# State-space output products four in a row, a contiguous tap table, whole-block input turns and kept low parts in a two-layer encoder trunk

## The chip, the core and the metric

The kernel runs on one core of a Trainium2 chip. Its engines work side by side and meet through semaphores: TensorE (PE) multiplies matrices into PSUM, VectorE (DVE), ScalarE (ACT) and GpSimd (POOL) do elementwise work, and SyncE (SP) issues the DMAs, in order, on one queue. The metric is the device time of one execution in microseconds (us); lower is better.

## What is computed

A trunk of two layers over a sequence of 1024 tokens with 1024 channels, all in float32. Layer 0 mixes tokens by an RWKV-7 recurrence (16 heads of 64), layer 1 by a diagonal complex state-space layer (S5; 64 groups of 16 channels, each with 64 complex states); each is followed by a dense MLP with squared ReLU, and after each of the four sub-layers the input is added with a factor and normalised. Cut to what matters here:

```python
def rwkv7_time_mix(x, ...):
    ...
    return (o.astype(x.dtype) * g) @ wo

def s5_mix(x, ...):
    ...
    def chunk_step(h, u_c):
        bu_re = jnp.einsum('tbgc,gpc->tbgp', u_c, bbar_re)
        bu_im = jnp.einsum('tbgc,gpc->tbgp', u_c, bbar_im)
            ...
        y = (jnp.einsum('tbgp,gcp->tbgc', s_re, cr_w)
             - jnp.einsum('tbgp,gcp->tbgc', s_im, ci_w))
        return (s_re[-1], s_im[-1]), y
    ...
    y = jax.nn.gelu(y + xf * d_skip)
    z = y @ w_glu
    return z[..., :d] * jax.nn.sigmoid(z[..., d:])

def sq_relu_mlp(x, w1, w2):
    return jnp.square(jax.nn.relu(x @ w1)) @ w2

for i in range(2):
    mix = rwkv7_time_mix(h, ...) if i == 0 else s5_mix(h, ...)
    h = layer_norm(DN_ALPHA * h + mix, ...)
    h = layer_norm(DN_ALPHA * h + sq_relu_mlp(h, ...), ...)
```

## The kernel before

**Layout and halves.** Activations lie with channels on the 128 partitions: 8 channel blocks of 128 (`KT`), and time along the free axis. The sequence is worked in two halves of 512 tokens (`HT`), H = 0 (tiles `hA`, operands `oAh`, `oAl`) and H = 1 (`hB`, `oBh`, `oBl`), so that one half's slow stages stand beside the other half's dense products.

**Dense products.** A float32 operand is split in a high part, rounded by a cast on ACT (L148), and a low part, the difference, on DVE (L149); each product is three PE instructions, high x high, high x low, low x high (`mm3`, issued at L188). `wload` (L162) brings 512 weight columns at a time: a load of 256 KB on SP into `wraw` (two buffers), the split into `whi` and `wlo` (three buffers each), and then 12 PE instructions use them. If a key is given, the first use stores the low part in DRAM (`low`, L180), and a later use loads it (L174) in place of the subtraction. The first half's projections in layer 0 do this for the second half's; the output projection `wo` (L950) has no key.

**Order.** The program is written stage by stage; a planner then orders each engine's instructions by a simulated timeline and by rank, a lower number first. The two MLPs of a half are written with a high number (from 200000), and the state-space layer with 99300 to 99500, so that the dense products of the other half's MLP fill what the state-space layer leaves free. The order on each engine is fixed when the kernel is built. PSUM has four pools with one 2 KB tile each per buffer: `pd` (three, dense products), `pl` (one), `pa` (two), `pc` (two).

**Tables.** `s5_tables` (L1026) makes, once, for each channel block `f` (8 groups in 4 pairs `g2`, two members `par`): `tB` (input to state), `tC` (state to output) and `tT`, the taps inside a stretch of 8 tokens. The taps of one block come from PE into `p` (L1151), ACT copies them into a zero-padded tile `kpad` (L1155), which holds (t, c, g), the pair index innermost, and two DMAs (L1159), one for each `par`, write the 8 shifted copies to `tT`.

**The state-space layer** `s5(H, h)` (L1173) has three stages.

- Input (L1180 to L1207). For a pair of channel blocks (`f2`, members `j`) the tokens are turned onto partitions: for each of 8 token positions `s` a block of 128 channels x 64 stretches is turned, by a transpose for `j` = 0 (L156) and a product with the identity for `j` = 1 (L154), both through `turn`, with every eighth token as the stationary operand. ACT copies to `u1`. Then, group by group, a transpose (L1195) brings (position, channel) onto partitions, ACT copies to `ug`, and products with `tB` (L1206) make the state inputs `hb`.
- Scan (L1209 to L1231): `advance` on DVE and POOL.
- Output (L1235 to L1268). For a pair of blocks the tables `tt` and `tcm` of both blocks are loaded into the four buffers of tag `tab`. For each `par`, one PSUM tile takes 8 tap products (L1250, 128 rows, moving operand `tv`, every fourth float of `tt`) and 16 state products (L1255, 64 rows given by `par`, 64 columns given by `j`); ACT copies it to `y1` (L1257). Transposes (L1263, into `pyt` of pool `pa`) turn it back, DVE adds the skip term (L1265), ACT applies the GELU (into `yg`, one buffer), and a DMA stores it for `glu`.

`glu` (L1007) then reads it back, and the next normalisation and MLP follow.

## Time and profile before

| | |
|---|---|
| median of 3 runs | 2742.12 us |
| lowest, highest | 2735.79, 2742.68 us |
| the profiled execution | 2746.6 us |
| its span, first to last instruction | 2744.8 us |
| mean granted clock of TensorE | 0.961 |

The profile is of one execution; instruction durations in the text are from it. A row of a timeline gives the start, the length from first start to last end, the engine, line, operation, operands (output <- inputs), the part of the array used (rows*columns), the shape, and the count. PE's instructions overlap, so the cost of a block of them is read from its start to the start of the next block. `PEld` is a weight load that runs beside products; `SPq` is a DMA issued by SP. A line such as "A <- B: 5.2, 2, 2.9" means that A waited for B 5.2 us in all, in 2 waits, 2.9 us the longest.

### The profile page before, as it was taken

To read this page: it belongs to the slowest core of one execution; us is meant where nothing else is said; L and a number is where in the kernel's file an instruction comes from. 1 tells how busy PE (TensorE), PEld (TensorE's weight loads), DVE (VectorE), ACT (ScalarE), POOL (GpSimd) and SP (SyncE) were. 2 spreads that over 40 slices of the span, in tenths; PEclk is the share of its full clock that TensorE was granted. 3 is DMA by queue.
4 is the path that set the end of the run, shared out by engine and by line. 5 is a ranking of instruction groups with operands and counts; after the bars stand their busy time and mean duration, and the time that the engine had idled before them with its cause. 6 is when DMAs were issued, how large, how long until landed. Compare 5 with 4: busy or idle time off the path is not lost.

```text
span 2744.8 us, 43807 instructions
## 1 busy us (share of the span) xinstructions
PE 2598.4 (95%) x16582; PEld 2089.9 (76%) x16582; DVE 1813.3 (66%) x3191; ACT 1154.8 (42%) x2038; POOL 630.6 (23%) x515
## 2 busy tenths in 40 slices
PE   7999979989899999989999999999999999999997
PEld 5778757678677777767876788778778887788886
DVE  7477677577786867997567553674855546755556
ACT  7455574544543333353532332434223324433334
POOL 3121542432442122342122000120220101210101
PEclk9989979999899999999999999999999999999998
DMA  4765455564223334545333533233343322333333
GB/s 146 235 214 175 151 164 156 178 203 142 81 86 88 93 92 148 141 129 163 100 112 127 174 95 100 81 96 112 103 164 110 96 96 81 119 96 96 96 96 100
DMA packets 215058, 345.90 MB, mean 126 GB/s; under 512 B 21184, under 2 KB 75584, under 8 KB 214848
## 3 DMA queue, kind: packets, MB, share of 16 engines
q1 hardware_dynamic: 214848, 343.10, 40.5%
q8 instruction: 131, 2.15, 0.3%
q14 instruction: 79, 0.65, 0.1%
HBM read 279.06 MB, written 63.96 MB: 125 GB/s over the span
## 4 chain that ended last, share of the span: by engine, by line
PE 44%; DVE 4%; issue 3%; DMA 1%; POOL 1%; ACT 1%; ACTq 0%; SPq 0%; DVEq 0%; POOLq 0%
PE d L188 39%; PE py L1250 1%; PE py L1255 1%; DVE wlo L149 1%; DMA wraw<-in_mw_dram 1%; PE pu L154 1%; PE pbu L1206 1%; POOL rl L975 1%; DVE hA L991 0%; DMA s_y<-yg 0%; DVE t L1218 0%; DVE hB L991 0%; ACT whi L148 0%; DVE sq L876 0%; PE pu L1195 0%
## 5 line engine op out<-in xcount | busy, mean ns | idle before, releaser
L148 ACT CAST whi<-wraw 128x512 fp32r<-128x512 f32 x668 | 413.5, 620 | 929.1 <-PE d L188 623.2
L149 DVE TENSOR_TENSOR wlo<-wraw,whi 128x512 fp32r<-128x512 f32 x668 | 500.6, 750 | 426.8 <-ACT whi L148 404.3
L188 PE MATMUL d<-qbuf,whi 128*128 128x512 f32 (+1 forms) x2112 | 657.0, 394 | 23.8 <-DVE hA L991 12.8
L188 PEld LDWEIGHTS d<-qbuf,whi 128*128 128x128 f32 x2112 | 391.8, 191 | 120.0 <-DVE hA L991 17.8
L188 PE MATMUL d<-qbuf,wlo 128*128 128x512 f32 (+1 forms) x1056 | 411.9, 392 | 10.7 <-DVE wlo L149 10.4
L975 POOL TENSOR_TENSOR rl<-rl 128x512 f32<-128x512 f32 x128 | 157.2, 1228 | 1094.5 <-ACT rl L974 1094.5
L188 PE MATMUL d<-oAh,whi 128*128 128x512 f32 (+1 forms) x960 | 390.9, 411 | 15.5 <-ACT ev L418 6.3
L188 PE MATMUL d<-oAl,whi 128*128 128x512 f32 (+1 forms) x960 | 387.5, 405 | 3.0 <-DVE oAl L149 2.8
L188 PE MATMUL d<-oAh,wlo 128*128 128x512 f32 (+1 forms) x960 | 386.5, 405 | 2.4 <-DVE wlo L149 2.3
L188 PE MATMUL d<-oBh,whi 128*128 128x512 f32 x704 | 279.2, 397 | 0.0
L188 PE MATMUL d<-oBh,wlo 128*128 128x512 f32 x704 | 278.7, 396 | 0.2 <-DVE wlo L149 0.2
L188 PE MATMUL d<-oBl,whi 128*128 128x512 f32 x704 | 277.1, 394 | 0.0
L188 PEld LDWEIGHTS d<-qbuf,wlo 128*128 128x128 f32 x1056 | 201.7, 191 | 56.5 <-DVE wlo L149 14.5
L188 PEld LDWEIGHTS d<-oAh,whi 128*128 128x128 f32 (+1 forms) x960 | 185.9, 194 | 62.2 <-ACT ev L418 8.4
L188 PEld LDWEIGHTS d<-oAh,wlo 128*128 128x128 f32 (+1 forms) x960 | 185.8, 194 | 44.4 <-DVE wlo L149 3.2
L188 PEld LDWEIGHTS d<-oAl,whi 128*128 128x128 f32 (+1 forms) x960 | 185.6, 194 | 43.1 <-DVE oAl L149 5.2
L991 DVE TENSOR_TENSOR hB<-hB,d 128x512 f32<-128x512 f32 (+1 forms) x256 | 165.0, 650 | 71.2 <-PE d L188 68.0
L991 DVE TENSOR_TENSOR hA<-hA,d 128x512 f32<-128x512 f32 x240 | 162.1, 682 | 64.4 <-PE d L188 62.1
L188 PEld LDWEIGHTS d<-oBh,wlo 128*128 128x128 f32 x704 | 132.9, 189 | 32.4 <-issue 2.0
L188 PEld LDWEIGHTS d<-oBl,whi 128*128 128x128 f32 x704 | 133.1, 189 | 29.9 <-issue 0.7
L188 PEld LDWEIGHTS d<-oBh,whi 128*128 128x128 f32 x704 | 133.1, 189 | 29.0 <-issue 1.2
L149 DVE TENSOR_TENSOR qbuf<-rl,qbuf 128x512 fp32r<-128x512 f32 x128 | 95.0, 742 | 73.5 <-ACT qbuf L148 73.5
(374 smaller groups left out, 3804.8 us busy)
## 6 DMA issues: line engine op xcount, KB each, us to landing
wraw<-in_mw_dram SPq DMA_DIRECT2D x520, 256.0 KB, 2.7
wraw<-in_glu_dram SPq DMA_DIRECT2D x64, 256.0 KB, 2.7
low<-wlo SPq DMA_DIRECT2D x52, 256.0 KB, 2.6
wlo<-low SPq DMA_DIRECT2D x52, 256.0 KB, 3.6
wraw<-in_wk_dram SPq DMA_DIRECT2D x32, 256.0 KB, 3.5
wraw<-in_wr_dram SPq DMA_DIRECT2D x32, 256.0 KB, 3.9
wraw<-in_wv_dram SPq DMA_DIRECT2D x32, 256.0 KB, 4.3
yl<-s_y SPq DMA_DIRECT2D x32, 256.0 KB, 3.1
```

The source lines that it names most:

```text
L148: S.copy(hi, src)
L149: (e or V).tensor_sub(lo, src, hi.bitcast(F32))
L154: PE.matmul(out, x, idt, start=True, stop=True)
L188: bulk.append((PE.matmul(p, w, x, **kw).ins, x.shape[-1]))
L975: G.tensor_mul(r, r, r)
L991: V.tensor_add(z, z, p)
L1206: PE.matmul(p[qs, g2, ri], tb[:, g2, ri, qs], u[:, 2 * g2 + par], start=True, stop=True)
L1250: PE.matmul(p[64 * j : 64 * j + 64, g2], ug[f][:, 2 * g2 + par], tv[:, par, g2], start=g2 == 0, stop=False, skip_group_check=True)
L1255: PE.matmul(p[64 * j : 64 * j + 64, g2], hb[qs, 4 * f + g2, ri, 0:NSC], tcm[qs, g2, ri], start=False, stop=ri == 1, skip_group_check=True)
```

## The change

Four things are changed.

1. Output products: for each pair of blocks the two `par` now have a PSUM tile each (one of pool `pc`, one of `pa`), all 16 tap products come first, and the 32 state products follow in an order in which `par` changes fastest, then `j`; `inorder` fixes that order for the planner. The turn back, `pyt`, goes to pool `pl`.
2. Tap table: `kpad` becomes two tiles of four blocks each, with the pair index outside, and `tT` is laid out so that the 128 taps of a group lie side by side. The stores come after every fourth block, 16 DMAs then.
3. Input: one block of 128 channels is turned four times as a whole, every fourth token as the stationary operand (128 of them), all by transposes; the second turn becomes two products per group, with the even and the odd columns of the identity (`sel`), each to one half of the PSUM partitions.
4. `wo` gives its weights a key, so the first half stores the low parts and the second half loads them.

```diff
--- before.py
+++ after.py
@@ -31,6 +31,7 @@
 LNG = (1, 3, 5)
 LNT = (2, 5)
 TB = 2
+TBF = 4
 LN8R = 400000
 MIXR = 100
 W0B = 5
@@ -126,6 +127,8 @@
     cmask = kp.tile([128, 8, L], F32, name="cmask")
     V.memset(cmask, 1.0)
     V.memset(cmask[:, :, 0:1], 0.0)
+    sel = cp.tile([128, 2, 64], F32, name="sel")
+    V.tensor_copy(sel, ident.rearrange("p (n e) -> p e n", e=2))
     mhalf = cp.tile([128, 64], F32, name="mhalf")
     V.memset(mhalf, -0.5)
 
@@ -180,6 +183,12 @@
                     SP.dma_start(low[key, k0], lo.bitcast(F32).rearrange("p k n -> p (k n)"))
             out += [(hi[:, k], lo[:, k]) for k in range(step)]
         return out
+
+    def inorder(prods):
+
+        for x, y in zip(prods, prods[1:]):
+            tc.add_manual_dep(y.ins, x.ins.name, mybir.DependencyInfo(
+                mybir.DependencyClass.NoSync, mybir.DependencyReason.DATA), reason="order")
 
     bulk, hops = [], []
     ST = getattr(nc, STE)
@@ -953,7 +962,7 @@
         hs = []
         for n in range(KT):
             p = psd()
-            dense(p, wload(A["wo"][n], KT, 128), ys)
+            dense(p, wload(A["wo"][n], KT, 128, f"wo{n}"), ys)
             h = htile(H)
             SP.dma_start(h, A["xT"][n * 128 : (n + 1) * 128, t0 : t0 + HT])
             V.scalar_tensor_tensor(h, h, ALPHA, p, op0=ALU.mult, op1=ALU.add)
@@ -1019,7 +1028,7 @@
 
     SL = 8
     NSC = HT // SL
-    tT = dr.tile([KT, 128, 2, 512], F32, name="tT")
+    tT = dr.tile([128, 2, KT, 4, 128], F32, name="tT")
     tB = dr.tile([KT, 128, 4, 2, 128], F32, name="tB")
     tC = dr.tile([KT, 128, 4, 2, 128], F32, name="tC")
 
@@ -1102,10 +1111,12 @@
         V.tensor_sub(ci, ci, tq)
         V.tensor_mul(ci, ci, den)
 
-        kpad = pp.tile([128, 16, 16, 4], F32, name="kpad")
-        G.memset(kpad, 0.0)
+        kpads = [pp.tile([128, TBF, 4, 16, 16], F32, name=f"kpad{j}") for j in range(KT // TBF)]
+        for kpad in kpads:
+            G.memset(kpad[:, :, :, 0:8], 0.0)
         for f in range(KT):
             gs = slice(4 * f, 4 * f + 4)
+            kpad = kpads[f // TBF]
             bc = pp.tile([128, 2, 2, 4, 16], F32, tag="bc", name="bc", bufs=1)
             SP.dma_start(bc, A["s5bc"][f])
             bb = pp.tile([128, 2, 4, 16], F32, tag="bb", name="bb", bufs=1)
@@ -1152,11 +1163,13 @@
                                   ca[ps_, g2, ri, 0:8].rearrange("p t c -> p (t c)"), start=ri == 0, stop=ri == 1)
             for par in range(2):
                 ps_ = slice(64 * par, 64 * par + 16)
-                S.copy(kpad[ps_, 8:].rearrange("p t c g -> p g (t c)"), p[ps_])
-            tv = tT[f].rearrange("(s c) two n -> two c s n", c=16)
-            for par in range(2):
-                src = kpad[64 * par : 64 * par + 16, 1:9].rearrange("p t c g -> p (t c g)")
-                SP.dma_start(tv[par], bass.AP(src.tensor, src.offset, [src.ap[0], (64, SL), src.ap[1]]))
+                S.copy(kpad[ps_, f % TBF, :, 8:].rearrange("p g t c -> p g (t c)"), p[ps_])
+            if f % TBF == TBF - 1:
+                for par in range(2):
+                    for s in range(SL):
+                        SP.dma_start(
+                            tT[16 * s : 16 * s + 16, par, f - TBF + 1 : f + 1].rearrange("c f g n -> c (f g) n"),
+                            kpad[64 * par : 64 * par + 16, :, :, 1 + s : 9 + s].rearrange("c f g t e -> c (f g) (t e)"))
 
             bs = pp.tile([128, 4, 2, 128], F32, tag="bs", name="bs", bufs=1)
             for hf in range(2):
@@ -1178,21 +1191,21 @@
             V.tensor_copy(hb[:, :, :, 0], carry[0])
         ug = []
         for f2 in range(4):
-            u1 = s5p.tile([128, 8, SL, 16], F32, tag="u1", name="u1", bufs=2)
-            for s2 in range(2):
+
+            u1 = s5p.tile([128, 2, 8, 4, 16], F32, tag="u1", name="u1", bufs=2)
+            for j in range(2):
                 p = pa.tile([128, 4, 128], F32, tag="a", name="pu1")
-                for j in range(2):
-                    src = h[2 * f2 + j].rearrange("p (c s) -> p c s", s=SL)
-                    for s in range(4):
-                        turn(p[64 * j : 64 * j + 64, s], src[:, :, SL - 1 - 4 * s2 - s], ident, j)
-                S.copy(u1[:, :, 4 * s2 : 4 * s2 + 4].rearrange("p g s c -> p s g c"),
-                       p.rearrange("p s (g c) -> p s g c", g=8))
+                src = h[2 * f2 + j].rearrange("p (m s) -> p s m", s=4)
+                for s in range(4):
+                    PE.transpose(p[:, s], src[:, 3 - s], ident)
+                S.copy(u1[:, j].rearrange("p g s c -> p s g c"), p.rearrange("p s (g c) -> p s g c", g=8))
             for j in range(2):
                 f = 2 * f2 + j
-                ps_ = slice(64 * j, 64 * j + 64)
                 p = pc.tile([128, HT], F32, tag="c", name="pu2").rearrange("p (g n) -> p g n", g=8)
                 for g in range(8):
-                    PE.transpose(p[:, g], u1[ps_, g].rearrange("p s c -> p (s c)"), ident[ps_, ps_])
+                    for e in range(2):
+                        PE.matmul(p[64 * (1 - e) : 64 * (1 - e) + 64, g], u1[:, j, g].rearrange("p s c -> p (s c)"),
+                                  sel[:, e], start=True, stop=True)
                 u = s5p.tile([128, 8, NSC], F32, tag="ug", name="ug", bufs=8)
                 S.copy(u, p)
                 ug.append(u)
@@ -1237,28 +1250,34 @@
             tabs = []
             for f in (2 * f2, 2 * f2 + 1):
                 tt = s5p.tile([128, 2, 512], F32, tag="tab", name="tt", bufs=4)
-                SP.dma_start(tt, tT[f])
+                SP.dma_start(tt.rearrange("p two (g n) -> p two g n", g=4), tT[:, :, f])
                 tcm = s5p.tile([128, 4, 2, 128], F32, tag="tab", name="tcm", bufs=4)
                 SP.dma_start(tcm, tC[f])
-                tabs.append((f, tt.rearrange("p two (n g) -> p two g n", g=4), tcm))
+                tabs.append((f, tt.rearrange("p two (g n) -> p two g n", g=4), tcm))
+
+
+            pp = [r.tile([128, HT], F32, tag=t, name="py").rearrange("p (g n) -> p g n", g=4)
+                  for r, t in ((pc, "c"), (pa, "a"))]
+            for g2 in range(4):
+                for par in range(2):
+                    for j, (f, tv, tcm) in enumerate(tabs):
+                        PE.matmul(pp[par][64 * j : 64 * j + 64, g2], ug[f][:, 2 * g2 + par], tv[:, par, g2],
+                                  start=g2 == 0, stop=False, skip_group_check=True)
+            prods = []
+            for g2 in range(4):
+                for ri in range(2):
+                    for j, (f, tv, tcm) in enumerate(tabs):
+                        for par in range(2):
+                            qs = slice(64 * par, 64 * par + 64)
+                            prods.append(PE.matmul(pp[par][64 * j : 64 * j + 64, g2], hb[qs, 4 * f + g2, ri, 0:NSC],
+                                                   tcm[qs, g2, ri], start=False, stop=ri == 1, skip_group_check=True))
+            inorder(prods)
             for par in range(2):
-                qs = slice(64 * par, 64 * par + 64)
-                p = pc.tile([128, HT], F32, tag="c", name="py").rearrange("p (g n) -> p g n", g=4)
-
-                for g2 in range(4):
-                    for j, (f, tv, tcm) in enumerate(tabs):
-                        PE.matmul(p[64 * j : 64 * j + 64, g2], ug[f][:, 2 * g2 + par], tv[:, par, g2],
-                                  start=g2 == 0, stop=False, skip_group_check=True)
-                for g2 in range(4):
-                    for ri in range(2):
-                        for j, (f, tv, tcm) in enumerate(tabs):
-                            PE.matmul(p[64 * j : 64 * j + 64, g2], hb[qs, 4 * f + g2, ri, 0:NSC], tcm[qs, g2, ri],
-                                      start=False, stop=ri == 1, skip_group_check=True)
-                S.copy(y1[:, :, :, par].rearrange("p t g c -> p g t c"), p.rearrange("p g (t c) -> p g t c", t=SL))
+                S.copy(y1[:, :, :, par].rearrange("p t g c -> p g t c"), pp[par].rearrange("p g (t c) -> p g t c", t=SL))
             for j in range(2):
                 f = 2 * f2 + j
                 js = slice(64 * j, 64 * j + 64)
-                p = pa.tile([128, SL, NSC], F32, tag="a", name="pyt")
+                p = pl.tile([128, HT], F32, tag="l", name="pyt").rearrange("p (t n) -> p t n", t=SL)
                 for t in range(SL):
                     PE.transpose(p[:, t], y1[js, t].rearrange("p g r c -> p (g r c)"), ident[js, js])
                 y = s5p.tile([128, HT], F32, tag="yg", name="yg", bufs=1)
```

## The prediction

> **What bounds the kernel now.** I read the page first (one core, so no comparison of cores), then a table of stages (busy time of each engine in stretches that I cut at the state-space layer), then TensorE's order of work inside those stretches, then the waits.
>
> ```profile
> span 2744.8 us, 43807 instructions
> PE 2598.4 (95%) x16582; PEld 2089.9 (76%) x16582; DVE 1813.3 (66%) x3191; ACT 1154.8 (42%) x2038; POOL 630.6 (23%) x515
> ```
>
> TensorE is busy for 95% of the span, 146.4 us idle; VectorE follows at 66%. A share is an average, so the stages decide. Columns of the table: stretch in us from the span's start, its length, busy us (and instructions) of PE, its weight loads, DVE, ACT, POOL, then granted clock, DMA share, GB/s.
>
> ```profile
> 1115.00:1270.00 155.00, 138.31 (x763) 104.63 (x762) 145.69 (x235) 67.00 (x102) 62.41 (x44) 0.93 0.54 142
> 1327.00:1403.00 76.00, 76.00 (x630) 61.59 (x629) 36.02 (x54) 33.24 (x57) 4.91 (x5) 1.00 0.35 108
> 1403.00:1481.00 78.00, 70.35 (x297) 53.35 (x295) 66.96 (x113) 20.06 (x34) 26.22 (x14) 0.96 0.30 95
> 1481.00:1545.00 64.00, 64.00 (x544) 48.93 (x544) 29.90 (x41) 23.02 (x38) 7.68 (x5) 0.99 0.65 223
> 1545.00:1660.00 115.00, 114.88 (x504) 94.09 (x503) 61.55 (x95) 37.39 (x64) 11.10 (x11) 1.00 0.34 99
> ```
>
> For the first half of the sequence: 1115 to 1270 builds the tables and finishes the second half's output projection, and there DVE is the full engine (145.69 of 155). 1327 to 1403 turns the input into groups, 1403 to 1481 is the scan (DVE 66.96 of 78), 1481 to 1545 makes the output `py`. In the input and output stretches PE is not idle, and in the 115 us after them only for 0.12: dense products of the MLP (L188) fill every hole, and the work behind is more of the same. So PE work removed from the input and output stretches shortens the run one for one; PE work removed from the scan becomes idle time. The second half repeats the three stretches some 530 us later.
>
> **The output products.** PE's order of work for one pair of channel blocks (start, length, line):
>
> ```profile
> 1489.03 0.65 PE L1250 MATMUL py<-tt,ug 128*64 128x128 f32 x2
> 1489.60 1.01 PE L1263 MATMUL pyt<-ident,y 64*128 64x64 f32 x16
> 1490.55 2.01 PE L1250 MATMUL py<-tt,ug 128*64 128x128 f32 x14
> 1492.49 1.96 PE L1255 MATMUL py<-tcm,hb 64*64 64x128 f32 x32
> 1494.38 2.01 PE L1250 MATMUL py<-tt,ug 128*64 128x128 f32 x16
> 1496.33 1.96 PE L1255 MATMUL py<-tcm,hb 64*64 64x128 f32 x32
> 1498.22 0.51 PE L188 MATMUL d<-oBh,whi 128*128 128x512 f32 x1
> ```
>
> The loops call 16 tap products (L1250) and 32 state products (L1255) for such a pair; the trace has 32 and 64, so one fp32 product is two PE instructions. From one start to the next block's start, the pair costs 0.57 us (1489.03 to 1489.60) and 7.67 us (1490.55 to 1498.22): 8.24 us. There are 4 pairs in each half, 8 in all.
>
> *State products.* 32 instructions take 1.89 us, 0.059 us each. They use 64 rows and 64 columns of the array, a quarter; the two blocks `j` alternate between column halves, the row half (`par`) stays for a whole block of 32. The change alternates rows too, with one PSUM tile per row half. Does PE then run four at once? Once in each half two blocks of L1255 follow each other directly, and a table of L1255 alone around the seam (stretch, length, PE busy and instructions, clock, DMA share, GB/s) shows it:
>
> ```profile
> 1482.10:1482.52 0.42, 0.42 (x12) 1.00 0.75 283
> 1482.80:1483.22 0.42, 0.42 (x20) 1.00 0.17 44
> ```
>
> Inside a block 12 instructions touch 0.42 us; where the end of one row half meets the start of the other, 20. Four are in flight under each 269 ns long instruction in the outer rows (a start each 0.055 us), so 4 of the counted 12 began earlier; at the seam twice the starts fall into the same time. So I price L1255 at half: 64 x 0.0295 = 1.9 us instead of 3.8.
>
> *Tap products.* L1250 uses all 128 rows and 64 columns, its two blocks also alternate columns, yet 16 instructions take 1.95 us, 0.122 each, twice as long as L1255's with the same 128 moving columns. What differs is that the moving table is read at every fourth float. The duration agrees, and the contiguous neighbour with the same 128 rows is L1206 (64 moving columns, two column halves):
>
> ```profile
> L1255 PE MATMUL py<-tcm,hb x512: 269/269/473, 1481.2 to 2057.2; 64*64 64x128 f32 x171
> L1250 PE MATMUL py<-tt,ug x256: 388/406/422, 1401.4 to 2055.1; 128*64 128x128 f32 x128
> 1343.73 2.09 PE L1206 MATMUL pbu<-ug,tb 128*64 128x64 f32 x64
> 1345.74 0.50 PE L188 MATMUL d<-oBl,whi 128*128 128x512 f32 x1
> ```
>
> L1206: 2.01 us / 64 = 0.031 for 64 columns, so 0.063 for 128. With the table contiguous I take 0.059 for L1250: 32 x 0.059 = 1.9 us. The bounds are 0.122 (no gain) and 0.055.
>
> The pair then costs 3.8 us instead of 8.24: 4.45 x 8 = 35.6 us of PE. But some of L1250 is run early, inside the scans, as fill (the same table, of L1250 alone):
>
> ```profile
> 1403.00:1481.00 78.00, 3.84 (x28) 0.96 0.30 95
> 1932.00:2010.00 78.00, 4.08 (x30) 0.96 0.30 97
> ```
>
> Half of 7.92 us saved there turns into idle time: 4.0. **Output products: -31.6 us.**
>
> **The input turn.** One of 8 chunks of a half now takes 4 transposes (L156) and 4 products (L154, 8 instructions):
>
> ```profile
> 1347.93 0.60 PE L156 MATMUL pu<-ident,hA 128*64 128x128 f32 x4
> 1348.46 1.23 PE L154 MATMUL pu<-ident,hA 128*64 128x128 f32 x8
> 1349.62 0.50 PE L188 MATMUL d<-qbuf,whi 128*128 128x512 f32 x1
> ...
> 1322.76 0.64 PE L888 MATMUL pr<-ident,rb 128*128 128x128 f32 x4
> 1323.15 0.48 PE L188 MATMUL d<-qbuf,whi 128*128 128x512 f32 x1
> ```
>
> That is 1.69 us x 8 = 13.5 us a half. The change makes 32 full transposes of strided blocks. No row shows one: four full contiguous ones (L888) take 0.39 us, 0.098 each; four strided ones that load half as many columns (L156) 0.53 us, 0.13 each. If the strided load sets that 0.13, twice the columns make it 0.26. I take 0.13, the strided row: 4.2 us a half, -9.3 (bounds -10.4 and -5.2). Both halves: **-18.6 us.**
>
> The second turn gets dearer: 16 transposes for a pair of blocks become 32 products, 64 instructions, of just L1206's form (2.01 us).
>
> ```profile
> 1337.99 1.01 PE L1195 MATMUL pu<-ident,u 64*128 64x64 f32 x16
> ```
>
> Sixteen of this form take 0.95 us from start to start (L1263 above, 1489.60 to 1490.55, is the same form). 2.01 - 0.95 = 1.06 us for each of 8 pairs: **+8.5 us.** It lies in the full stretch and is paid. ACT's copies are as many as before.
>
> **The way out and the tables.** `pyt` moves to a pool with one buffer, so its second set of transposes waits for VectorE's 1.2 us on the first.
>
> ```profile
> L1265 DVE SCALAR_TENSOR_TENSOR yg<-hA,pv,pyt x8: 1164/1188/1266, 1490.3 to 1539.9; 128x512 f32<-128x512 f32 x8
> ```
>
> PE can put dense products between, as it does everywhere in this stretch; if it can't, 8 x 1.19 = 9.5. I take +1.5, near zero, for the two sets that now run apart. The table stores, 16 now, become 32 of half the size in two bursts of 16, each at 0.36 us on SP's queue, in front of weight loads (in the second row the last number is us from issue to landing):
>
> ```profile
> L1159 SPq DMA_DIRECT2D tT<-kpad x16: 320/362/1264, 1128.6 to 1268.9; - x16
> tt<-tT SPq DMA_DIRECT2D x16, 512.0 KB, 4.2
> ```
>
> A burst holds SP 5.8 us, about two weight loads' worth of dense work; +1 (0 to 11.6). ACT's copies behind them write contiguous rows now, off the path. The table loads (4.2 us) stay of the same size, but the output stretch that carries them is shorter, so they crowd: 223 GB/s over 64 us are 14.3 MB, now in about 48 us, 298 GB/s. Holding the 283 of the first seam row would cost 2.5 us a half; I take +2 for both (0 to 5; all of it at 223, a rival).
>
> **The output projection.** The first half stores 16 low parts (16 more DMAs on SP), the second loads them in place of 16 subtractions on VectorE. Columns: count | busy, mean ns | idle; and for waits total us, times, longest.
>
> ```profile
> L149 DVE TENSOR_TENSOR wlo<-wraw,whi 128x512 fp32r<-128x512 f32 x13 | 11.0, 847 | 0.0
> ...
> PE d L188 <- DVE wlo L149: 5.2, 2, 2.9
> ...
> SPq L174 <- PE d L188: 62.8, 29, 9.9
> SPq L180 <- DVE wlo L149: 47.4, 23, 6.8
> ...
> PE d L188 <- DMA wlo<-low: 0.5, 1, 0.5
> ```
>
> The first row is 1115 to 1165, where this projection meets the tables on the full DVE, the second PE's wait there in 1115 to 1270. I take the 5.2 us that PE visibly waits: **-5** (bounds: 0, and the 11.0 of DVE work). The last three are whole-span rows of the 52 weights that do this already: SP stands still at a load until PE frees a buffer, at a store until DVE is done, and weight loads queue behind; but PE lost only 0.5 us to it. Stores in the first half: +1 (0 to 5).
>
> **Sum:** -31.6 - 18.6 + 8.5 + 1.5 + 1 + 2 - 5 + 1 = -41.2 us. The profiled execution took 2746.6 us (span 2744.8 and 1.8 around it), 4.5 above the median of the runs shown; I subtract from the median: 2742.1 - 41.2 = **2701 us**.
>
> **The rivals.**
> 1. *Products stay in strict order.* If a tile's second instruction holds up the next tile's first, four in a row run as two: +1.9 x 8 = 15, 2716. The seam (20 against 12) speaks against it, so 0.08. [...]
> 2. *The stride is not what slows the tap products.* Then L1250 stays at 0.122: +2 x 8 = 16, 2717. L1206's 0.031 speaks against.
> 3. *Tables and weights don't come fast enough.* If the output stretch can't beat the 223 GB/s measured there, 14.3 MB take their 64 us again and all 16 us a half come back: 2733. For it: the buffers hold one pair's tables, so each pair waits for its loads (4.2 us). Against: the DMA share is 0.65 there, so 298 GB/s would be 0.87, and a short stretch showed 283.
> 4. *The order is planned anew and the gain is given back* in the attention core, where PE has idle time already: 2736, no change. Nothing in the profile points there, but every part of the order may move.
> 5. *Slower: SP's queue.* 32 new waits like the last rows': 16 stores at 47.4/23 = 2.1 us and 16 loads at 62.8/29 = 2.2, all passed on to PE, make 68 us: 2701 + 68 + 5 = 2774. It decides from about 46 us, two thirds of that. Against: the 0.5 us.
>
> **How the numbers follow.** Forecast (2686 to 2712) 0.65; rivals 0.08, 0.07, 0.08, 0.05, 0.07. The range leaves out rivals 3 to 5 (0.20) and takes in the bounds of the turns, the table bursts and the small terms: 2682 to 2724. About 0.3% (8 us) is what a measurement of this kernel can tell from no change: so 2733 lies on the edge and counts half to either side: faster 0.65 + 0.15 + 0.04 = 0.84, same 0.09, slower 0.07.
>
> **What would show it.** The pair of output blocks takes about 3.8 us of PE; L1255 starts four instructions each 0.11 us; L1250's median falls from 406 ns towards L1255's 269; the output stretches shrink by some 15 us each with PE still full; the input stretch by about 5; PE's busy time falls by some 40 us and its idle time hardly. PE idle inside the output stretch would speak for rival 3, waits on `low` for rival 5. I'd be wrong first of all if PE's idle time, 146.4 us, grew by as much as its work shrank.

## The result, and the profile after

| | before | after |
|---|---|---|
| median of the runs, us | 2740.39 (6 runs) | 2759.88 (6 runs) |
| ratio to before, 95% interval | | 1.0071 (1.005 to 1.0091) |
| profiled execution, us (span) | 2746.6 (2744.8) | 2759.87 (2758.2) |

The changed kernel is slower by 0.5 to 0.9%. The forecast was 2701 us (2682 to 2724): the side and the range were both wrong. In the experiments below, one execution of e16 (2884 us at granted clock 0.826) and one of the kernel before beside it (4923 us) were in a slow state and are left out of the ratio. (In this part line numbers are the changed kernel's: dense products L188 are now L197, state products L1255 are L1272, tap products L1250 are L1264, the table store L1159 is L1170, the weight load is L172 and the load of a low part L177. The experiments shift some by a few lines; the tiles' names stay.)

The page of the changed kernel:

```profile
span 2758.2 us, 44350 instructions
...
PE 2568.4 (93%) x16838; PEld 2078.2 (75%) x16838; DVE 1808.8 (66%) x3176; ACT 1146.0 (42%) x2038; POOL 624.6 (23%) x516
```

TensorE's busy time fell from 2598.4 to 2568.4 us, so the work did shrink; its idle time (span less busy) grew from 146.4 to 189.8. The 30.0 us won went into idle time and 13.4 more with them. This is the case that the prediction named as the first that would make it wrong.

Where PE's work shrank, TensorE's order of work in the changed kernel shows (start, length, line; idle time before it in brackets):

```profile
1354.84 1.12 PE L1200 MATMUL pu<-ident,hA 128*128 128x128 f32 x8
1357.17 1.15 PE L1207 MATMUL pu<-sel,u 128*64 128x64 f32 x32 [1.21 <-ACT u L1201]
1358.25 0.72 PE L197 MATMUL d<-qbuf,whi 128*128 128x512 f32 x2
...
1498.14 1.98 PE L1272 MATMUL py<-tcm,hb 64*64 64x128 f32 x64
1500.05 0.74 PE L197 MATMUL d<-qbuf,whi 128*128 128x512 f32 x2
...
1507.54 1.96 PE L1264 MATMUL py<-tt,ug 128*64 128x128 f32 x28
1509.43 0.43 PE L1272 MATMUL py<-tcm,hb 64*64 64x128 f32 x2
1509.79 0.71 PE L1282 MATMUL pyt<-ident,y 64*128 64x64 f32 x8
1510.43 1.97 PE L1272 MATMUL py<-tcm,hb 64*64 64x128 f32 x62
```

A pair's 64 state products take 1.91 us from start to the next start, 28 tap products 1.89 (0.0675 each, 2.16 for the 32). The pair's products cost 4.07 us where they cost 8.24: 4.17 x 8 = 33.4 us less. Eight whole-block transposes take 1.12 us (their length, since PE is idle behind them), 0.14 each: 64 of them 9.0 us in place of 27.0. The second turn takes 1.08 us for 32, 2.16 for a pair in place of 0.95: 9.7 us more; `pyt` 0.64 for 8, 1.28 in place of 0.95: 2.6 more. Sum -39.1 us, close to what was predicted for these parts.

Where the time went, two rows of the table of stages show, cut into 1100 to 1330 us (tables and output projection) and 1330 to 2100 (state-space layers of both halves). The columns are those of the prediction's table: stretch, length, then busy us and instructions of PE, weight loads, DVE, ACT, POOL, then clock, DMA share, GB/s. Before:

```profile
1100.00:1330.00 230.00, 210.97 (x1095) 163.18 (x1094) 205.72 (x346) 97.26 (x153) 80.73 (x58) 0.96 0.49 136
1330.00:2100.00 770.00, 753.18 (x4390) 598.61 (x4389) 458.42 (x699) 271.40 (x463) 126.43 (x89) 0.99 0.37 117
```

After:

```profile
1100.00:1330.00 230.00, 183.66 (x959) 139.30 (x958) 171.22 (x296) 72.50 (x125) 67.16 (x51) 0.91 0.52 146
1330.00:2100.00 770.00, 734.34 (x4710) 594.44 (x4709) 480.18 (x716) 282.28 (x482) 129.23 (x96) 0.98 0.36 117
```

PE's idle time (length less busy) grew from 19.0 to 46.3 us in the first stretch and from 16.8 to 35.7 in the second. In the first, the timeline of SP in the changed kernel shows the two bursts of table stores:

```profile
1162.98 0.41 SPq L172 DMA_DIRECT2D wraw<-in_mw_dram  x1
1163.44 19.41 SPq L1170 DMA_DIRECT2D tT<-kpad  x16
1182.95 1.33 SPq L1181 DMA_DIRECT2D tB<-bs  x1
...
1258.46 19.30 SPq L1170 DMA_DIRECT2D tT<-kpad  x16
1277.86 1.21 SPq L1181 DMA_DIRECT2D tB<-bs  x1
```

A burst of 16 stores holds SP 19.4 us, 1.2 each, not the 5.8 of the forecast. No weight load leaves SP in that time, and the waits of TensorE in 1100 to 1330 us (total us, times, longest) show who pays: a split that waits for its weights, and a low part behind the burst.

```profile
PE d L197 <- ACT whi L151: 22.8, 3, 20.7
PE d L197 <- DMA wlo<-low: 11.3, 1, 11.3
```

In the last 10 us of the second burst nothing runs at all but the stores (table of stages of the changed kernel):

```profile
1268.00:1277.80 9.80, 0.00 (x0) 0.00 (x0) 0.00 (x0) 0.00 (x0) 0.00 (x0) 0.50 0.75 101
```

The DMA engines are 75% busy there and move only 101 GB/s; in the output stretch they are 66% busy and move 230 (row 1498 to 1560, shown below). The engines are occupied, but with stores that go slowly.

In the second stretch the waits of TensorE (1330 to 2100 us) after the change are

```profile
PE py L1264 <- DMA tt<-tT: 10.6, 4, 3.2
PE d L197 <- DVE hB L1000: 9.3, 5, 4.0
PE d L197 <- DVE hA L1000: 8.9, 5, 4.0
PE pu L1207 <- ACT u L1201: 3.1, 2, 1.9
```

and before

```profile
PE d L188 <- DVE wlo L149: 5.3, 3, 2.2
PE d L188 <- DVE hA L991: 4.4, 6, 1.2
PE d L188 <- DVE hB L991: 4.0, 7, 1.1
```

The tap products now wait for their table, and dense products wait twice as long for VectorE's additions. Three stretches of the first half, to set beside the rows of before (input, scan, output):

```profile
1352.00:1420.00 68.00, 66.79 (x726) 55.09 (x726) 32.32 (x49) 32.46 (x55) 4.19 (x4) 1.00 0.37 117
1420.00:1498.00 78.00, 70.28 (x326) 55.79 (x322) 69.31 (x114) 20.05 (x34) 21.46 (x13) 0.93 0.29 92
1498.00:1560.00 62.00, 55.01 (x541) 43.50 (x541) 33.26 (x44) 23.60 (x40) 9.32 (x6) 0.94 0.66 230
```

The output stretch, full before (64.00 of 64.00), now has 7.0 us of idle time.

### The profile page after: what moved, and what is told of

Same layout as the page of the kernel before. It is cut to its first block, busy times and chain, and to the rows that moved or that the text cites. A ratio compares the mean times of both kernels' runs of the same rounds, so it can differ in the third digit from the quotient of the medians.

```text
span 2758.2 us, 44350 instructions
## 1 busy us (share of the span) xinstructions
PE 2568.4 (93%) x16838; PEld 2078.2 (75%) x16838; DVE 1808.8 (66%) x3176; ACT 1146.0 (42%) x2038; POOL 624.6 (23%) x516
## 4 chain that ended last, share of the span: by engine, by line
PE 56%; DVE 14%; DMA 6%; issue 5%; ACT 3%; POOL 2%; SPq 2%; ACTq 0%; DVEq 0%; POOLq 0%
PE d L197 50%; DVE wlo L152 2%; SPq L1170 1%; DMA wraw<-in_mw_dram 1%; PE pA L605 1%; DMA yl<-s_y 1%; DMA ldr<-s_r 1%; DMA s_y<-yg 1%; DVE hA L1000 1%; PE pu L1207 1%; ACT whi L151 1%; PE pbu L1219 1%; DVE xh L650 1%; DVE qbuf L152 1%; DVE x L648 1%
## 5 line engine op out<-in xcount | busy, mean ns | idle before, releaser
L151 ACT CAST whi<-wraw 128x512 fp32r<-128x512 f32 x652 | 404.1, 620 | 942.0 <-PE d L197 692.0
L152 DVE TENSOR_TENSOR wlo<-wraw,whi 128x512 fp32r<-128x512 f32 x652 | 492.6, 757 | 420.2 <-ACT whi L151 403.9
L197 PE MATMUL d<-qbuf,whi 128*128 128x512 f32 (+1 forms) x2112 | 659.1, 395 | 32.2 <-DVE hA L1000 16.0
L197 PEld LDWEIGHTS d<-qbuf,whi 128*128 128x128 f32 x2112 | 394.3, 192 | 127.0 <-DVE hA L1000 24.2
L197 PE MATMUL d<-oAh,whi 128*128 128x512 f32 (+1 forms) x960 | 393.3, 413 | 38.6 <-ACT whi L151 21.1
L197 PE MATMUL d<-qbuf,wlo 128*128 128x512 f32 (+1 forms) x1056 | 412.5, 393 | 5.8 <-DVE wlo L152 5.6
L984 POOL TENSOR_TENSOR rl<-rl 128x512 f32<-128x512 f32 x128 | 147.9, 1156 | 1147.9 <-ACT rl L983 1143.6
L197 PE MATMUL d<-oAl,whi 128*128 128x512 f32 (+1 forms) x960 | 388.3, 406 | 2.2 <-DVE oAl L152 2.0
L197 PE MATMUL d<-oAh,wlo 128*128 128x512 f32 (+1 forms) x960 | 387.1, 406 | 1.2 <-DVE wlo L152 1.2
L197 PE MATMUL d<-oBh,wlo 128*128 128x512 f32 x704 | 278.9, 397 | 11.3 <-DMA wlo<-low 11.3
L197 PE MATMUL d<-oBh,whi 128*128 128x512 f32 x704 | 279.8, 397 | 0.0
L197 PE MATMUL d<-oBl,whi 128*128 128x512 f32 x704 | 277.9, 395 | 0.0
L197 PEld LDWEIGHTS d<-oAh,whi 128*128 128x128 f32 (+1 forms) x960 | 186.6, 195 | 84.5 <-ACT whi L151 22.0
L197 PEld LDWEIGHTS d<-qbuf,wlo 128*128 128x128 f32 x1056 | 202.6, 192 | 50.8 <-DVE wlo L152 8.9
L197 PEld LDWEIGHTS d<-oAl,whi 128*128 128x128 f32 (+1 forms) x960 | 186.9, 195 | 42.7 <-DVE oAl L152 4.3
L197 PEld LDWEIGHTS d<-oAh,wlo 128*128 128x128 f32 (+1 forms) x960 | 186.2, 194 | 42.9 <-DVE wlo L152 1.9
L197 PEld LDWEIGHTS d<-oBh,wlo 128*128 128x128 f32 x704 | 133.3, 189 | 44.3 <-DMA wlo<-low 11.9
L197 PEld LDWEIGHTS d<-oBl,whi 128*128 128x128 f32 x704 | 133.4, 189 | 30.2 <-issue 1.3
L197 PEld LDWEIGHTS d<-oBh,whi 128*128 128x128 f32 x704 | 133.5, 190 | 28.1 <-issue 0.6
```

The source lines that it names most:

```text
L151: S.copy(hi, src)
L152: (e or V).tensor_sub(lo, src, hi.bitcast(F32))
L197: bulk.append((PE.matmul(p, w, x, **kw).ins, x.shape[-1]))
L984: G.tensor_mul(r, r, r)
```

## The experiments

Two theories at first. **The stores**: the two bursts of table stores hold up the weights, and cost some 28 us. **The products**: something in the new order of products or in the kept low parts (the prediction's rival 5) costs it. PE's idle time in the table is worked out as above from two rows of the table of stages of each run.

| kernel | median, us | ratio to before (95%) | PE idle 1100-1330 | 1330-2100 |
|---|---|---|---|---|
| e1 all but the table part | 2732.95 | 0.9976 (0.9961 to 0.999) | 22.2 | 25.1 |
| e4 table part alone | 2760.23 | 1.0084 (1.0057 to 1.0112) | 39.3 | 22.3 |
| e5 four products in a row alone | 2739.89 | 1.0 (0.9988 to 1.0013) | 19.5 | 30.4 |
| e6 whole-block turns alone | 2736.95 | 0.9986 (0.9971 to 1.0) | 21.7 | 18.7 |
| e7 kept low parts alone | 2736.96 | 1.0 (0.9982 to 1.0018) | 22.9 | 15.9 |
| e2 bursts of half the size | 2735.15 | 0.9997 (0.9985 to 1.001) | 27.0 | 37.7 |
| e11 stores issued by POOL | 2753.16 | 1.0041 (1.0025 to 1.0057) | 37.0 | 39.2 |
| e16 halves on two queues | 2746.85 | 1.0019 (1.0002 to 1.0036) | 39.6 | 37.2 |
| e17 halves alternate | 2743.89 | 1.0001 (0.9984 to 1.0018) | 33.7 | 37.8 |
| e3 taps contiguous by 16, stores as before | **2723.87** | **0.9938 (0.9916 to 0.996)** | 21.9 | 34.5 |
| e12 e3, `tt` ahead of `tcm` | 2724.68 | 0.9936 (0.9923 to 0.9948) | 21.9 | 35.0 |
| e15 e12, `pyt` in two buffers | 2732.42 | 0.998 (0.9967 to 0.9993) | 20.1 | 40.0 |
| e13 e3, `yg` from shared buffers | 2853.6 | 1.0409 (1.0395 to 1.0424) | 24.8 | 146.1 |
| e14 e12 and e13 together | 2837.95 | 1.0342 (1.0326 to 1.0359) | 24.8 | 125.8 |

**Which part costs.** e1 is the changed kernel with the table of before: tile, stores and load.

```diff
-            if f % TBF == TBF - 1:
-                for par in range(2):
-                    for s in range(SL):
-                        SP.dma_start(tT[16 * s : 16 * s + 16, par, f - TBF + 1 : f + 1]..., kpad[...])
+            tv = tT[f].rearrange("(s c) two n -> two c s n", c=16)
+            for par in range(2):
+                src = kpad[64 * par : 64 * par + 16, 1:9].rearrange("p t c g -> p (t c g)")
+                SP.dma_start(tv[par], bass.AP(src.tensor, src.offset, [src.ap[0], (64, SL), src.ap[1]]))
```

> The change without its table part: the strided table of before, stored after every block in two DMAs; the other three parts stay. Theory A (the two bursts of 16 table stores hold back the weight loads): the 28 us lost between 1160 and 1300 come back and the tap products cost their 16 us again, 2760 - 28 + 16 = 2748 us. Theory B (the waits of the output projection's kept low parts on SP's queue do it): the loss stays and the taps cost more, about 2776 us.

e4 is the opposite, the kernel before with the table part alone (the same diff the other way round); e7 has the kept low parts alone:

```diff
-            dense(p, wload(A["wo"][n], KT, 128), ys)
+            dense(p, wload(A["wo"][n], KT, 128, f"wo{n}"), ys)
```

> Before with the table part alone (contiguous taps, two bursts). Theory A: 2740 + 28 - 16 (tap products at half) = 2752 us, PE idle between 1160 and 1300 as in the changed kernel. Theory B: no loss there, 2724 us.

> Before with the kept low parts of the output projection alone. Theory A: 2735 to 2741 us, as the prediction had it (-5 +1). Theory B: 2755 us or more, with PE waiting for low.

Taking the table part away brings the ratio from 1.0071 to 0.9976, 0.0095 or 26 us, and PE's idle time of the first stretch back to 22.2; that part alone makes the kernel before 0.84% slower. e1 came out faster than expected (2733 us, not 2748). The strided taps are not free, though: e3 below, which differs from e1 only in the order of the floats in the table, is faster by another 0.0038, 10 us. So the bursts cost the run more than these 26 us, some 36. The kept low parts change nothing that can be measured: the new waits on SP (rival 5, 68 us) don't come, and the 5 us hoped for don't either. The theory of the products falls as the cause of the loss.

**Why the stores cost.** e2 halves a burst (`TBF = 4` becomes `TBF = 2`: four bursts of 16 stores with 64 KB); e11 moves the stores to POOL's queue, so that SP stays free:

```diff
-                        SP.dma_start(
+                        G.dma_start(
                             tT[16 * s : 16 * s + 16, par, f - TBF + 1 : f + 1]...
```

> The change with TBF = 2: the same 512-byte rows and the same bytes, in four bursts of 16 stores of 64 KB in place of two of 128 KB. Theory A: a burst of some 8 us is about as long as the weights that lie ready, so most of the 28 us come back, 2735 to 2745 us. Theory B: unchanged, 2760 us.

> The changed kernel with the 32 table stores issued by POOL instead of SP; sizes, rows and times of the bursts stay. If the loss is SP's queue standing still (each store keeps SP for 1.35 us and the weight loads stand behind it), it goes: about 2735 us. If the loss is the 16 DMA engines full of 512-byte rows, which the weight loads need whatever queue issues them, most of it stays: 2750 to 2760 us.

The second and the fourth burst of e2 on SP:

```profile
1158.58 9.39 SPq L1170 DMA_DIRECT2D tT<-kpad  x16
...
1243.81 9.66 SPq L1170 DMA_DIRECT2D tT<-kpad  x16
```

Half the bytes, half the time, and nearly the whole loss of the first stretch is gone (27.0 us idle against 22.2 without the table part). Bursts of 9.4 us are ridden out with the weights already loaded, bursts of 19.4 aren't. With POOL issuing, SP is free and most of the loss stays. POOL's timeline in e11:

```profile
1165.71 5.42 POOL L1170 DMA_DIRECT2D tT<-kpad  x9
1171.70 0.56 POOL L1170 DMA_DIRECT2D tT<-kpad  x1 [0.57 <-DMA tT<-kpad]
...
1179.88 0.56 POOL L1170 DMA_DIRECT2D tT<-kpad  x1 [0.33 <-DMA tT<-kpad]
```

After nine issues POOL, too, goes on only as earlier stores land. So it isn't SP's issuing that is slow: the data is.

What makes it slow? A burst is 16 x 128 KB = 2.1 MB; in 19.41 us that is 108 GB/s. In the table of stages it is 101 GB/s where nothing else moves (1268 to 1277.8 us, above). Rows of 512 bytes are not it: the stores of the kernel before, with rows of 2 KB, go at such a rate as well. A row of its table of stages, from just behind two of its stores:

```profile
1192.00:1197.00 5.00, 2.92 (x15) 2.08 (x13) 5.00 (x6) 4.33 (x8) 5.00 (x5) 1.00 0.65 92
```

The two stores of 256 KB are alone here, and the row takes in some time at its end in which they have landed; cut from 1191.0 to 1195.8 us it reads 107 GB/s. Both kinds read 16 partitions of `kpad` at a time. e16 and e17 test that: they change neither bytes nor rows, only which of the 32 stores are under way together.

```diff
-                        SP.dma_start(
+                        (SP, G)[par].dma_start(
```

That is e16, one half on each queue; e17 keeps SP and turns the two loops:

```diff
-                for par in range(2):
-                    for s in range(SL):
+                for s in range(SL):
+                    for par in range(2):
```

> Starts from the changed kernel (2759.9 us, ratio 1.0071; a burst of 2 MB holds SP 19.4 us, 108 GB/s; PE idle from 1100 to 1300 us 46.2 us). Only the queue of half of the table stores is changed: the 8 of a burst that read kpad's partitions 0 to 15 stay on SP, the 8 that read partitions 64 to 79 are issued by POOL, so that both halves are under way together. Theory P, what limits a store is that it reads 16 partitions only: the two halves run beside each other, SP is held some 10 us, the idle time falls to about 28 us and the run to about 2740 (ratio 1.000). Theory D, the DMA engines as a whole move rows of this kind at 100 GB/s whichever partitions they come from: SP's 8 stores still take 16 to 20 us, weights still wait, 2750 to 2760 as with all stores on POOL (ratio 1.0041).

> Starts from the changed kernel (2759.9 us); all 32 table stores stay on SP, but the two halves of kpad's partitions alternate store by store (before: 8 of the first half, then 8 of the second). Theory P with several stores in flight at once: a burst takes 10 to 12 us in place of 19.4 and the run comes to about 2740. Theory P with the stores of one queue served strictly one after the other, or theory D: no change, 19 us and 2755 to 2762.

The two bursts of e17 on SP:

```profile
1158.01 12.93 SPq L1170 DMA_DIRECT2D tT<-kpad  x16
...
1245.96 12.61 SPq L1170 DMA_DIRECT2D tT<-kpad  x16
```

With nothing but the order changed, a burst takes 12.9 us in place of 19.4 (162 GB/s), and some 19 us of the run come back (ratio 1.0071 to 1.0001). Had the DMA engines as a whole set the rate, the order would not matter. e16 stands between the two expectations: SP's eight stores take 16.3 us.

```profile
1164.48 16.34 SPq L1170 DMA_DIRECT2D tT<-kpad  x8
```

POOL had issued its own eight by 1170.8 us, so both halves were under way together, and yet the DMA engines moved only 122 GB/s (1168 to 1180 us), where the changed kernel moves 101 (1168 to 1182) and e17 175 (1162 to 1170). Two queues gain a fifth, the alternating order on one queue three quarters. So theory P, two halves that simply run beside each other, is not the whole account, and why e16 gains so little stays open. Nor is it shown that the partitions read are the cause: turning the loops also changes which rows of DRAM are written together, and no run separates the two. That the old stores, which write the table in another layout, go as fast speaks for the partitions.

One number fits four kernels: call the weights in hand x us, a burst of b us costs PE b - x. Idle time above the 22.2 us of e1, shared among the bursts: after 24.1 / 2, so x = 19.35 - 12.05 = 7.3; e16 17.4 / 2, x = 16.25 - 8.7 = 7.5; e17 11.5 / 2, x = 12.8 - 5.75 = 7.0; e2 4.8 / 4, x = 9.65 - 1.2 = 8.4 (9.65 is the mean of its four bursts, 9.22 to 10.31). So TensorE has seven to eight us of weights in hand, by this estimate. A burst of 5.8 us, as predicted, would by it have cost nothing. (e11 isn't of this form; there SP goes on issuing.)

**The parts that should have won.** e3 keeps every part of the change but writes the table differently: `kpad` is ordered (t, g, c), stored in two stores after each block as before, and the tap products read runs of 16 contiguous floats. Its table, set against that of the kernel before:

```diff
-        kpad = pp.tile([128, 16, 16, 4], F32, name="kpad")
+        kpad = pp.tile([128, 16, 4, 16], F32, name="kpad")
...
-                tabs.append((f, tt.rearrange("p two (n g) -> p two g n", g=4), tcm))
+                tabs.append((f, tt.rearrange("p two (t g c) -> p two g t c", g=4, c=16), tcm))
```

e5 and e6 have one part each on the kernel before: four products in a row (with the two tiles `pp` and `inorder`), and the whole-block turns with `sel`.

> All four parts, but the table keeps its two stores of 2 KB rows after every block: the padded tile holds (t, g, c), so a shifted copy is one contiguous stretch as before, and the tap products read runs of 16 contiguous floats instead of single floats 16 bytes apart. Theory A (512-byte rows in bursts cost the 28 us, the stride costs the taps): no loss between 1160 and 1300 and L1250 at about 273 ns; 2733 (the kernel with the old table) - 18 + some 4 given back in the output stretch = 2719 us. Rival: it is the change of layout as such, or the taps need full contiguity: 2733 us or more.

> Before with four in a row alone (old table, old turns). PE work falls by 14 us (state products at half). If PE work in the output stretch is worth its time: 2726 us. If the output stretch is by now set by its table loads and by the single output buffer, the work comes back as idle time: 2735 us or more.

> Before with the whole-block turns alone. PE work falls by 18 - 10 = 8 us. If PE work in the input stretch is worth its time: 2730 us. If the scan behind it takes the time back (its dense work waits for VectorE): 2736 us or more.

e3 beats both kernels, by 0.4 to 0.8% against the kernel before. Its tap products take the 273 ns (median) of the changed kernel's, not the 407 of e1's strided ones (the tile's instructions in e3: min/median/max ns), and its first stretch is as full as e1's:

```profile
L1260 PE MATMUL py<-tt,ug x256: 272/273/324, 1383.4 to 2029.5; 128*64 128x128 f32 x128
```

But 16.7 us faster is less than half of the 39 us by which the products and turns shrink. The rest is idle time of the second stretch: 34.5 us where the kernel before has 16.8. e5 shows it undiluted: the state products shrink there as in the changed kernel (256 of them, from 1330 to 1580 us, are busy for 9.2 us; 8.8 in the changed kernel, 16.2 before), PE's busy time over the whole span falls by 12.2 us (2586.2 against 2598.4), and 13.6 us more of idle time stand in the second stretch (30.4 less 16.8), ratio 1.0. In e6 the idle time of that stretch hardly grows (18.7), and the ratio is 0.9986, with an interval that reaches no change. The rows of that stretch in e3 and in e5:

```profile
1330.00:2100.00 770.00, 735.46 (x4698) 595.61 (x4697) 473.93 (x708) 271.74 (x465) 122.97 (x91) 0.98 0.37 119
1330.00:2100.00 770.00, 739.58 (x4373) 585.22 (x4372) 460.32 (x693) 266.21 (x457) 135.52 (x89) 0.99 0.36 116
```

**What the idle time of the output stretch waits for.** The letters of these four expectations are their own. In e3 both table loads of a pair are issued block by block, so the second block's `tt` stands on SP behind a `tcm` that waits for its buffer.

```diff
+            tts = []
             for f in (2 * f2, 2 * f2 + 1):
                 tt = s5p.tile([128, 2, 512], F32, tag="tab", name="tt", bufs=4)
                 SP.dma_start(tt, tT[f])
+                tts.append(tt)
+            for f, tt in zip((2 * f2, 2 * f2 + 1), tts):
                 tcm = s5p.tile([128, 4, 2, 128], F32, tag="tab", name="tcm", bufs=4)
```

> Starts from e3 (2723.9 us); only the order of the four table loads of a pair is changed: both tt ahead of both tcm. Theory A, a queue effect: tcm of the first block waits for a buffer that the state products of the pair before still read, and tt of the second block stands behind it on SP, so TensorE waits for tt (11.2 us in 1300 to 2100 us of e3). Then the waits for tt fall below 4 us and the run to about 2717. Theory B, the single output buffer yg sets the pace: no change, 2724. Theory C, any wait removed there is replaced by the next (tcm, hb, pu): waits for tt fall, others rise by as much, 2721 to 2727.

TensorE's waits in e12, 1330 to 2100 us:

```profile
PE d L197 <- DVE hB L1000: 10.1, 6, 3.8
PE d L197 <- DVE hA L1000: 8.4, 5, 3.7
PE pyt L1281 <- DVE yg L1283: 6.8, 3, 3.9
PE pyt L1281 <- ACT y L1275: 3.1, 2, 1.6
```

The 11.2 us of waits for `tt` that e3 has are gone, 9.9 us of `pyt` have come (its single buffer, and ACT's copy), and the time is the same. e15 gives `pyt` two buffers again (`p = pa.tile([128, SL, NSC], F32, tag="a", name="pyt")`, as before the change):

> Starts from e12 (ratio 0.9936); pyt goes back to the pool with two buffers, as in the kernel before. In e12 the waits for tt (11.2 us) were gone and 10 us of waits of pyt, for its only buffer (6.8) and for ACT's copy of y (3.1), stood in their place. If the single pyt buffer is what came next, TensorE's waits in 1300 to 2100 us fall by 7 us and the ratio to about 0.991 (2717 us on the scale of e3). If the waits stand in for one another (theory C: VectorE's output step with the single yg, or dense products waiting for VectorE in the scan, come next), the ratio stays at 0.992 to 0.995 and TensorE's idle time of 1300 to 2100 us within 4 us of e3's 34.2.

```profile
PE py L1263 <- DMA tt<-tT: 11.2, 4, 3.8
PE d L197 <- DVE hB L1000: 6.5, 6, 2.9
PE d L197 <- DVE hA L1000: 6.4, 3, 4.7
PE pyt L1281 <- ACT y L1275: 4.8, 3, 2.1
```

The `tt` waits are back although `tt` is still asked for first, and the run is slower than e12. The edit isn't clean: pool `pa` now also holds one of the two `py` tiles, which it didn't before the change, so `pyt` and `py` share its two buffers. What e12 and e15 show is that waits stand in for one another here: asking for `tt` earlier doesn't shorten the run, nor does this second buffer for `pyt`. The third candidate, VectorE waiting 20.5 us for the single `yg` to be stored in the changed kernel, was to be tried with `yg` from the three buffers of the evictions:

```diff
-                y = s5p.tile([128, HT], F32, tag="yg", name="yg", bufs=1)
+                y = tp.tile([128, HT], F32, tag="ev", name="yg", bufs=3)
```

> Starts from e3 (2723.9 us); the output tile yg is taken from the three shared buffers of the evictions instead of its own single one. Theory B, the single buffer sets the pace of the output stretch: VectorE's idle time before L1280 (waits for s_y<-yg, some 20 us in the changed kernel) falls below 8 us and the run to about 2717. Theories A and C: VectorE's wait goes and TensorE's idle time of 1400 to 2100 us stays, 2721 to 2727.

> Starts from e3 (2723.9 us) with both edits, tt ahead of tcm and yg from the shared buffers. If the two waits are separate and each is paid, the gains add: about 2711. If the waits stand in for one another (theory C), 2718 to 2727, and TensorE's idle time in 1300 to 2100 us falls by less than 5 us against e3.

Both failed as tests. The edit moved the order itself: in e3 4444 dense products run ahead of the first state product (at 1465.9 us), in e13 3928 (at 1383.0), so TensorE arrives at them while the scan still runs and can do nothing else:

```profile
PE py L1268 <- DVE hb L1231: 75.3, 2, 38.0
PE pyt L1278 <- ACT y L1272: 39.3, 8, 9.7
```

The run is 130 us longer, with 112 us more of idle time in this stretch. About `yg` it says nothing, and a second buffer of its own was not tried.

## Why the prediction was wrong

**The step that failed: "A burst holds SP 5.8 us ... +1 (0 to 11.6)".** It priced a store at the 0.36 us that SP's issue took in the kernel before, where two stores stand alone between other work. In a burst of 16 a store held SP for 1.2 us (19.41 / 16), and with POOL issuing, in e11, POOL stood 10.7 us in 13 waits for earlier ones to land. The bytes were the right base: 2.1 MB at the 107 GB/s of the old stores are 19.6 us, and 19.4 were measured. With seven us of weights in hand, two such bursts make some 24 us of idle time by the estimate above, and the run pays more: e3, which differs from the changed kernel in its table alone, is faster by 0.0133 of the time, 36 us (its idle time, 162.7 us, is 27.1 less, and its PE is busy 10.5 us less). So about 36 of the 59 us between 2701 and 2760 are this term, forecast at +1. The bound of 11.6 was both bursts at the same wrong price, not a bound from another row.

**Output products, -31.6: the second step that failed.** The work is right: -33.4 measured less some give-back. The state products, four in a row, started twice as fast as two in a row: 64 in 1.91 us (predicted 1.9), before 32 in 1.89. So rival 1, with its 2716, falls. The stride was what slowed the taps, so rival 2 falls too: 0.0675 us each contiguous, against 0.122. What failed is the premise, "PE work removed from the input and output stretches shortens the run one for one". e5 took 12.2 us of PE work away, got 13.6 us of idle time and no gain. In e3, without the bursts, 23 us are still missing from 2701; the idle time of 1330 to 2100 us, 17.7 above the kernel before, and the 5 us that the output projection didn't give make up about as much (a sum, not a test).

**Crowding of the table loads, +2, and the 4.0 given back in the scans: mis-sized.** The idle time of 1330 to 2100 us grew by 18.9 us: 10.6 of it stand as waits for `tt`, 9.8 as longer waits for VectorE's additions into `hA` and `hB` (18.2 against 8.4); waits for low parts fell from 5.3 to 0.8. Rival 3 saw the right stretch (the loads, "each pair waits") and was given 0.08; that asking for the table earlier doesn't help by itself, e12 shows.

**The input turn, -18.6, and the second turn, +8.5**: -18.0 and +9.7, right. **`pyt`, +1.5**: +2.6 of work, and its single buffer comes up as a wait only where `tt` is early (e12). **The output projection, -5**: 0 in e7; in the changed kernel one load of a low part even stood 11.3 us behind the burst. **Rival 4**, the gain given back in the attention core: no; the idle time ahead of 1100 us isn't larger (84.5 us, before 87.0). **Rival 5** ended on the right side for the wrong reason: SP's queue was the place, but the stores of the table filled it, not the low parts.

Put together: work -39.1, idle time +27.3 and +18.9, and about 6 us more make the 13.4 us between the two spans. The dense products may be these six: their 9328 records are busy for 2185.4 us where they were for 2178.8, and those just behind the second burst (1277.8 to 1290 us, granted clock 0.50) take 0.41 us each, against 0.24 in the 40 us after them (0.99). e4, the other kernel with these bursts, has 2184.3; e1 and e3, without them, 2171.6 and 2176.6. No run tests this by itself.

**What stays open** is what sets the pace of the output stretch, now that its products take half the time. The order of the table loads alone doesn't (e12); e15 speaks against the single `pyt` buffer, but shares its two buffers with `py`; the single `yg` and VectorE's additions are untested. Open too is what makes a store of 16 partitions slow, and why alternating on one queue helps more than two queues.

## What to carry to other kernels

Price a burst of DMAs by bytes over the rate that this kind of transfer reaches in the trace (here some 100 GB/s for stores that read 16 partitions, with rows of 512 bytes and of 2 KB alike), not by the issue time of one that stands alone, and hold its length against the weights that are already loaded. A stretch in which an engine is full proves that work removed there is not waiting now; it doesn't prove that the next bound is far, so look for the waits just behind before counting a saving one for one. When a re-layout helps the reader of a table, look for the form that leaves its writer alone: here runs of 16 floats brought the tap products from 406 ns to the 273 of contiguous ones with the old stores.

## What the runs showed of the hardware that was not expected

- The order of equal stores on one queue changed their rate by half: 16 stores of 128 KB took 19.4 us with the two groups of source partitions one after the other, 12.9 us with the groups alternating. With one group on each of two queues, SP's eight alone took 16.3 us.
- The taps did not need full contiguity as a moving operand: with runs of 64 bytes they took 273 ns (median, e3), as long as contiguous ones (273, changed kernel); at every fourth float they took 406 (kernel before).
- While TensorE stood still for lack of weights (its longest wait there 20.7 us) its granted clock fell: 0.50 in the empty 1268 to 1277.8 us of the changed kernel, 0.91 over 1100 to 1330, where the kernel before has 0.96. The clock was still 0.50 over the first dense products behind the gap (1277.8 to 1290 us), which took 0.41 us each, against 0.24 in the 40 us after them (0.99).
